# Seven-product down projection: the last weight block is copied aside, the raw buffers are released after the second e split, and the next up weights are summed behind the accumulations

## The chip, the cores and the metric

The kernel runs on one core of a Trainium2 chip. The metric is the device time of one execution in microseconds (us). Three runs of the kernel before took 1870.8, 1871.56 and 1874.53 us; the median is 1871.56 us. All rows below come from one profiled execution, with times counted from the start of its span.

A core has five engines with a queue of instructions each: TensorE (PE in the rows, with PEld for its weight loads), VectorE (DVE), ScalarE (ACT), GpSimd (POOL) and SyncE (SP). Each takes its queue in order, and an instruction whose inputs are not there holds up everything behind it on its engine. DMA transfers are issued from SP and POOL here and run on 16 DMA engines.

## The reference

One layer of an encoder on two groups of tokens (512 and 256, behind 16 shared meta tokens), in float32:

```python
def swiglu(u, wg, wu, wd):
    return (jax.nn.silu(u @ wg) * (u @ wu)) @ wd

h = h + 0.5 * swiglu(rmsnorm(h, ffn1_norm_w[layer]), ffn1_w_gate[layer], ffn1_w_up[layer], ffn1_w_down[layer])
...
h = h + jnp.concatenate([att, ssm], axis=-1) @ w_out[layer]
h = h + 0.5 * swiglu(rmsnorm(h, ffn2_norm_w[layer]), ffn2_w_gate[layer], ffn2_w_up[layer], ffn2_w_down[layer])
h = rmsnorm(h, final_norm_w)
```

The model width is 1024, the hidden width of the two SwiGLU blocks 2816. The change touches only the second one, where 768 tokens are left: some 500 us at the end of the kernel.

## The kernel before, in words

**Precision.** Every float32 weight is split into a rounded part (hi) and a rest (lo): ScalarE makes hi by a cast (L202), VectorE subtracts it from the weight (L203). A product is three matmuls: hi·hi (L372), lo·hi (L373), hi·lo (L374).

**Seven products.** The projections of the second SwiGLU are 2 x 2 block products done with seven block products, which need sums of weight blocks. One "quad" is such a block product for a pair of 128 hidden columns of gate or of up: seven steps, called here by their functions p1, p6, p5, p2, p7, p3, p4, each of 12 matmuls of 128 x 384. A quad takes two raw pieces of the weights and four split jobs: `a` (one block as it is), `b` (sums made by VectorE at L277 and L278 out of both raw pieces), `c` (a whole piece), `d` (sums at L282 and L283).

**Groups.** The hidden columns are worked in groups of two pairs. The down projection of a group is done in the middle of the next group: after the gate quad of that group's first pair comes `down_fast` for the group before, then the up quad. There are four such places, called stages 1 to 4 below. A `down_fast` goes twice over two column pairs (`cq` = 0 and 2). Each round has the products b11, b21, t2, m3, n1, b22, m4 (12 matmuls each). ScalarE puts PSUM results aside (`put`, L783), VectorE adds others to them (`fold`, L786), and each fold is followed by a DMA from POOL that adds 128 x 384 values to the residual in DRAM (L788). m4 goes on in the PSUM bank of m3 (a `ps_x` bank), so it may begin only when the fold of the m3 result has read that bank. The split jobs of a round are `e0`, `e1` (four blocks each) and `f0`, `f1` (three blocks each); f needs sums made with e, and the raw block r22.

**What sets the order.** The list `jobs` fixes the order of all weight splits, `raws_in` that of the loads: in `cq` = 2 the jobs are e0, e1, f0, f1 and then a, b, c, d of the up quad. There are two raw buffers (tag `wr`, 512 KB per load, issued from SP at L229) and four hi/lo buffers (tags `wh`, `wl`). `split` issues the next loads when a job was the last to read its raw piece; `pump` lets at most four splits run ahead of the buffers that products have freed. A recording layer then sets the instructions of each engine in a fixed order.

Of the kernel before, what the change touches and what calls it, by code (L numbers as in the profile page):

```python
# [47 lines left out]
def body(tc, x_prompt, x_sample, meta_tokens, ffn1_norm_w, ffn1_w_gate, ffn1_w_up, ffn1_w_down,  # L48
# [125 lines left out]
    def plan_down_fast(f, wd, g):  # L174
        for cq in range(0, KD // 2, 2):
            a = len(raws_in)
            for kind in "ef":
                for i in range(2):
                    jobs.append(((f, "d", g, cq + i, kind), kind + str(i), (a + i,)))
            raws_in.extend((wd, 2 * GROUPS[f][g], 4, (cq + i) * 256, 256) for i in range(2))  # L180
# [36 lines left out]
    class Weights:  # L217
        raw, ready = {}, {}
        n_dma = n_split = n_got = n_free = n_used = 0
# [16 lines left out]
        def split(self):  # L236
            j = self.n_split
            key, kind, rs = jobs[j]
            while self.n_dma <= max(rs):
                self.dma()  # L240
# [20 lines left out]
        def split_fast(self, key, kind, raw, hi, lo):  # L261
# [6 lines left out]
            if kind[0] in "ef":  # L268
                return self.split_down(key, kind, raw[0], hi, lo)
            hv, lv = (t.rearrange("p a b -> p (a b)").rearrange("p (s k f) -> p s k f", s=2, k=4) for t in (hi, lo))  # L270
            if kind == "a":
                ins = split(hv[:, 0], lv[:, 0], raw[0][:, :, x])
            else:
                if kind == "b":
                    sums = stretch_pool[0].tile([P, 2 * 4 * P], F32, tag="sums", name="sums", bufs=1)
                    t = self.sums = sums.rearrange("p (s k f) -> p s k f", s=2, k=4)
                    V.tensor_tensor(t[:, 1], raw[0][:, :, y], raw[1][:, :, y], ALU.add)  # L277
                    V.tensor_tensor(t[:, 0], t[:, 1], raw[0][:, :, x], ALU.add)  # L278
                else:

                    t, self.sums = self.sums, None
                    V.tensor_tensor(t[:, 1], raw[0][:, :, x], raw[0][:, :, y], ALU.add)  # L282
                    V.tensor_tensor(t[:, 0], t[:, 0], raw[1][:, :, x], ALU.add)  # L283
                ins = split(hv, lv, t)
# [3 lines left out]
        def split_down(self, key, kind, r, hi, lo):  # L288

            x, y = slice(0, P), slice(P, 2 * P)  # L290
            r11, r12, r21, r22 = r[:, 0:2, x], r[:, 2:4, x], r[:, 0:2, y], r[:, 2:4, y]
            hv, lv = (t.rearrange("p a b -> p (a b)").rearrange("p (s k f) -> p s k f", s=4, k=2) for t in (hi, lo))
            odd = kind[1] == "1"
            if kind[0] == "e":
# [14 lines left out]
                split(hv[:, 2:4], lv[:, 2:4], s23)  # L309
                n = 4  # L310
            else:
                ins = split(hv[:, 0:2], lv[:, 0:2], self.sumb if odd else self.sums[:, 2:4])
                split(hv[:, 2], lv[:, 2], r22)
                n = 3
# [3 lines left out]
            return ins  # L318

        def pump(self, most=1):  # L320
            while most and self.n_split < min(len(jobs), self.n_free + NHL):
                self.split()
                most -= 1
# [227 lines left out]
    def ffn(f, h, halves, norm, after, last, new_g, new_up, first, parts=None, rms=None, ended=None, kept=None):  # L551
# [219 lines left out]
        def down_fast(g, late):  # L771
# [13 lines left out]
            def fold(t, src, m, hf):  # L785
                V.scalar_tensor_tensor(t, src[:, :n0], 0.5, t, ALU.mult, ALU.add)  # L786
                o, n = halves[hf]
                G.dma_start(out=kept[m][:, o:o + n], in_=t, accum_op=ALU.add)  # L788

            for cq in range(0, KD // 2, 2):  # L790
                two = range(2)
                e = [W.get((f, "d", g, cq + i, "e")) for i in two]
                m0 = [2 * (cq + i) for i in two]
# [33 lines left out]
                for i in two:  # L827
                    z.append(ps_mm())
                    prod(z[i], fs[i][1], "b22")
                    fold(c12[i], z[i], m0[i], 1)  # L830
                    done()
# [1075 lines left out]
```

## Time and profile before

| | |
|---|---|
| median of three runs | 1871.56 us |
| profiled execution, own time | 1870.07 us |
| its span, first to last instruction | 1868.3 us |
| TensorE busy | 1787.5 us (96%) |
| VectorE busy | 1353.1 us (72%) |
| ScalarE busy | 850.0 us (45%) |

The profiled execution is 1.5 us shorter than the median of the runs. TensorE is busy nearly throughout, so what counts is where it is not, and where its granted clock is below full speed (a lower clock counts as busy). A row of a timeline has the start, the length, the engine, the line, the operation, output and input names, and in square brackets how long the engine sat idle before it and what ended that.

### The profile page before, as it was taken

Reading aid. Unit: us, or ns where it says so; the run is one execution under the profiler, and the core shown is the slowest. Engines: PE = TensorE matmul, PEld = TensorE weight load, DVE = VectorE, ACT = ScalarE, POOL = GpSimd, SP = SyncE. Lnnn points to the kernel's source line nnn. Section 1 sums busy time; section 2 is a strip of 40 time slices with the busy share of each in tenths; the row PEclk is TensorE's granted clock in tenths of the full one; section 3 lists DMA queues with packets and bytes.
Section 4 is the critical chain, followed back from the end, with each engine's and each line's share of the span. In section 5 each row is a group of like instructions: output and inputs, shape, how many; then the busy total and the mean of one; then the engine's idle time right before and its main releaser. Section 6 shows DMA issues by size and latency. Waiting matters only on the chain. (4 is left out here: it accounts for less than half of the span.)

```text
span 1868.3 us, 27750 instructions
## 1 busy us (share of the span) xinstructions
PE 1787.5 (96%) x10622; PEld 1708.1 (91%) x10622; DVE 1353.1 (72%) x2679; ACT 850.0 (45%) x1700; POOL 159.0 (9%) x198
## 2 busy tenths in 40 slices
PE   8999999999999999998999999999999898989898
PEld 7999999999999987887988989999999898989897
DVE  6857858585864796767787887756878585858663
ACT  6513414142433535766476764533435353434434
POOL 0000000000020000323000000003001102020302
PEclk9999999999999999998999999999999999999999
DMA  4212212121232525965432135221232525262631
GB/s 142 74 46 74 80 54 83 48 88 46 91 116 60 155 82 141 258 184 160 149 103 72 60 126 188 80 68 46 76 103 72 122 76 116 68 124 68 147 124 68
DMA packets 171767, 188.65 MB, mean 101 GB/s; under 512 B 11201, under 2 KB 155706, under 8 KB 171634
## 3 DMA queue, kind: packets, MB, share of 16 engines
q1 hardware_dynamic: 161122, 168.00, 29.9%
q0 software_dynamic: 10496, 18.88, 5.3%
q8 instruction: 83, 1.36, 0.3%
q14 instruction: 50, 0.41, 0.1%
q10 hardware_dynamic: 16, 0.00, 0.0%
HBM read 151.68 MB, written 38.60 MB: 102 GB/s over the span
## 5 line engine op out<-in xcount | busy, mean ns | idle before, releaser
L372 PE MATMUL ps_mm<-w,wh 128*128 128x384 f32 (+4 forms) x1200 | 408.9, 341 | 9.3 <-DVE f L679 2.8
L373 PE MATMUL ps_mm<-w,wl 128*128 128x384 f32 (+4 forms) x1200 | 405.9, 338 | 1.5 <-DVE wl L203 1.5
L374 PE MATMUL ps_mm<-w,wh 128*128 128x384 f32 (+4 forms) x1160 | 393.6, 340 | 2.7 <-DVE w L203 2.2
L202 ACT CAST wh<-wr 128x512 fp32r<-128x512 f32 (+1 forms) x210 | 182.2, 867 | 182.5 <-PE ps_x L374 90.6
L203 DVE TENSOR_TENSOR wl<-wr,wh 128x512 fp32r<-128x512 f32 (+1 forms) x210 | 210.4, 1002 | 54.8 <-ACT wh L202 53.2
L372 PEld LDWEIGHTS ps_mm<-w,wh 128*128 128x128 f32 x1200 | 226.4, 189 | 17.9 <-issue 4.5
L373 PEld LDWEIGHTS ps_mm<-w,wl 128*128 128x128 f32 x1200 | 226.3, 189 | 4.7 <-DVE wl L203 2.2
L374 PEld LDWEIGHTS ps_mm<-w,wh 128*128 128x128 f32 x1160 | 218.7, 189 | 7.5 <-DVE w L203 3.0
L202 ACT CAST wh<-sums 128x1024 fp32r<-128x1024 f32 (+1 forms) x100 | 94.7, 947 | 201.3 <-DVE sums L278 85.5
L372 PE MATMUL ps_x<-w,wh 128*128 128x392 f32 (+4 forms) x432 | 150.4, 348 | 22.2 <-DVE f L786 21.3
L372 PE MATMUL ps_s<-w,wh 128*128 128x384 f32 (+1 forms) x432 | 148.7, 344 | 9.7 <-DVE f L673 7.5
L373 PE MATMUL ps_x<-w,wl 128*128 128x392 f32 (+4 forms) x432 | 147.8, 342 | 0.0
L373 PE MATMUL ps_s<-w,wl 128*128 128x384 f32 (+1 forms) x432 | 147.2, 341 | 0.0
L374 PE MATMUL ps_s<-w,wh 128*128 128x384 f32 (+1 forms) x432 | 146.8, 340 | 0.0
L203 DVE TENSOR_TENSOR wl<-sums,wh 128x1024 fp32r<-128x1024 f32 (+1 forms) x100 | 109.6, 1096 | 42.3 <-ACT wh L202 42.2
L374 PE MATMUL ps_x<-w,wh 128*128 128x392 f32 (+4 forms) x392 | 134.5, 343 | 0.0
L421 POOL TENSOR_TENSOR w<-w,w 128x392 f32<-128x392 f32 (+3 forms) x36 | 41.7, 1160 | 1009.7 <-ACT w L420 1009.7
L372 PEld LDWEIGHTS ps_x<-w,wh 128*128 128x128 f32 x432 | 84.6, 196 | 25.6 <-DVE f L786 22.9
L372 PEld LDWEIGHTS ps_s<-w,wh 128*128 128x128 f32 x432 | 82.2, 190 | 14.3 <-DVE f L673 9.8
L373 PEld LDWEIGHTS ps_x<-w,wl 128*128 128x128 f32 x432 | 84.6, 196 | 0.7
L373 PEld LDWEIGHTS ps_s<-w,wl 128*128 128x128 f32 x432 | 82.0, 190 | 0.0
L374 PEld LDWEIGHTS ps_s<-w,wh 128*128 128x128 f32 x432 | 81.8, 189 | 0.0
(408 smaller groups left out, 3951.1 us busy)
## 6 DMA issues: line engine op xcount, KB each, us to landing
wr<-in_ffn_w_gate_dram SPq DMA_DIRECT2D x44, 512.0 KB
wr<-in_ffn_w_up_dram SPq DMA_DIRECT2D x42, 512.0 KB
wr<-in_w_in_dram SPq DMA_DIRECT2D x42, 512.0 KB
wr<-in_ffn_w_down_dram SPq DMA_DIRECT2D x40, 512.0 KB
w<-ar_d SPq DMA_DIRECT2D x24, 512.0 KB
wr<-in_w_out_dram SPq DMA_DIRECT2D x16, 512.0 KB
w<-ar_d SPq DMA_DIRECT2D x24, 256.0 KB
w<-q_d SPq DMA_DIRECT2D x32, 192.0 KB
```

The lines of the kernel that those rows point to most:

```text
L202: a = S.copy(hi, src)
L203: return a, V.tensor_tensor(lo, src, hi.bitcast(F32), ALU.subtract)
L372: nc.tensor.matmul(ps, ah, bh, start=start, stop=False, skip_group_check=onto)
L373: nc.tensor.matmul(ps, al, bh, start=False, stop=False, skip_group_check=onto)
L374: last_mm[0] = nc.tensor.matmul(ps, ah, bl, start=False, stop=stop, skip_group_check=onto)
L421: G.tensor_tensor(sums[0], sums[0], sq, ALU.add)
```

## The change

It has two parts, and both stand in `down_fast` and its weight splits.

First, the raw pieces of a round are needed by e0 and e1 alone. After e1, ScalarE copies the two raw blocks r22 (128 x 256 each) into the sums tile, in the place of sums that are split by then, and the f jobs split r22 from there. The f jobs name no raw piece any more; the piece of e0 is kept until the copies.

Second, in the round `cq` = 2 the job `b` of the next up quad is held back until both c12 folds are recorded, and its first addition is told to stand behind the second of them.

```diff
@@ plan_down_fast
-                    jobs.append(((f, "d", g, cq + i, kind), kind + str(i), (a + i,)))
+                    rs = ((a,), (a, a + 1))[i] if kind == "e" else ()
+                    jobs.append(((f, "d", g, cq + i, kind), kind + str(i), rs))
@@ Weights.split
-            while self.n_dma <= max(rs):
+            while rs and self.n_dma <= max(rs):
@@ Weights.split_fast
-                return self.split_down(key, kind, raw[0], hi, lo)
+                return self.split_down(key, kind, raw[-1] if raw else None, hi, lo)
...
                 if kind == "b":
+                    if self.behind:
+                        kept_order = behind([self.behind])
+                        self.behind = None
+                    else:
+                        kept_order = ExitStack()
                     sums = stretch_pool[0].tile([P, 2 * 4 * P], F32, tag="sums", name="sums", bufs=1)
                     t = self.sums = sums.rearrange("p (s k f) -> p s k f", s=2, k=4)
-                    V.tensor_tensor(t[:, 1], raw[0][:, :, y], raw[1][:, :, y], ALU.add)
+                    with kept_order:
+                        V.tensor_tensor(t[:, 1], raw[0][:, :, y], raw[1][:, :, y], ALU.add)
@@ Weights.split_down
                 split(hv[:, 2:4], lv[:, 2:4], s23)
                 n = 4
+                self.r22.append(r22)
+                if odd:
+                    for i in range(2):
+                        S.copy(s23[:, i], self.r22[i])
+                    self.r22 = []
             else:
                 ins = split(hv[:, 0:2], lv[:, 0:2], self.sumb if odd else self.sums[:, 2:4])
-                split(hv[:, 2], lv[:, 2], r22)
+                split(hv[:, 2], lv[:, 2], self.sums[:, int(odd)])
@@ Weights.pump
-            while most and self.n_split < min(len(jobs), self.n_free + NHL):
+            while most and self.n_split != self.hold and self.n_split < min(len(jobs), self.n_free + NHL):
@@ down_fast
             for cq in range(0, KD // 2, 2):
                 two = range(2)
+                if cq:
+                    W.hold = W.n_got + 5
...
-                    fold(c12[i], z[i], m0[i], 1)
+                    W.behind = fold(c12[i], z[i], m0[i], 1)
+                    if i:
+                        W.hold = None
                     done()
```

In the rows of the changed kernel the lines have moved: L203 is L205, L277 and L278 are L285 and L286, L282 and L283 are L290 and L291, L673 is L692, L679 is L698, L689 is L708, L697 is L716, L783 is L802, L786 is L805.

VectorE, second round of stage 1, from the c11 folds (`f<-ps_s`) on; `f<-ps_x` are the folds of the m3 results, `w<-ps_mm` the c12 folds, `w<-ps_x` the folds of m4; `wl<-wr 128x512` is the lo part of the up quad's `a`, and the sums are those of its `b` and `d`. Before:

```order
L786 SCALAR_TENSOR_TENSOR f_14271<-ps_s,f_14271 128x384 x2
L277 TENSOR_TENSOR sums<-wr 128x512
L278 TENSOR_TENSOR sums<-sums,wr 128x512
L203 TENSOR_TENSOR wl<-wr,wh 128x512
L203 TENSOR_TENSOR wl<-sums,wh 128x1024
L786 SCALAR_TENSOR_TENSOR f_14342<-ps_x,f_14342 128x384 x2
L786 SCALAR_TENSOR_TENSOR w_14343<-ps_mm,w_14343 128x384
L282 TENSOR_TENSOR sums<-wr 128x512
```

Now:

```order
L805 SCALAR_TENSOR_TENSOR f_14275<-ps_s,f_14275 128x384 x2
L205 TENSOR_TENSOR wl<-wr,wh 128x512
L805 SCALAR_TENSOR_TENSOR f_14339<-ps_x,f_14339 128x384 x2
L805 SCALAR_TENSOR_TENSOR w_14340<-ps_mm,w_14340 128x384 x2
L285 TENSOR_TENSOR sums<-wr 128x512
L805 SCALAR_TENSOR_TENSOR w_14306<-ps_x,w_14306 128x384
L286 TENSOR_TENSOR sums<-sums,wr 128x512
L805 SCALAR_TENSOR_TENSOR w_14306<-ps_x,w_14306 128x384
L205 TENSOR_TENSOR wl<-sums,wh 128x1024
L205 TENSOR_TENSOR wl<-wr,wh 128x1024
L290 TENSOR_TENSOR sums<-wr 128x512
L291 TENSOR_TENSOR sums<-sums,wr 128x512
```

The sums of `b`, which need both raw pieces of the up weights, stood ahead of the m3 folds and stand behind the c12 folds now; one lo part, which needs the first raw piece, is ahead of the m3 folds still.

ScalarE, the same round, from the last three puts of the first round (`cq` = 0) to the first of the second (`w<-ps_s` and `f<-ps_s` are puts, the casts those of e1, f0 and f1 of `cq` = 2). Now:

```order
L802 ACTIVATE f_14205<-ps_s 128x384
L204 CAST wh<-sums 128x512
L802 ACTIVATE w_14206<-ps_s 128x384
L324 COPY sums<-wr 128x256 x2
L204 CAST wh<-sums 128x512
L204 CAST wh<-sums 128x256
L204 CAST wh<-sumb 128x512
L204 CAST wh<-sums 128x256
L802 ACTIVATE f_14275<-ps_s 128x384 x2
```

The two copies stand between the last put of the first round and the casts of the f jobs, whose 128x256 ones read `sums` where they read `wr`.

VectorE a little later in stage 1, in the up quad; L673/L692 takes up the result of p6, L679/L698 that of p5, L689/L708 that of p2, and the last `wl<-wr 128x512` and `sums<-wr` belong to `a` and `b` of the next gate quad. Before:

```order
L203 TENSOR_TENSOR wl<-sums,wh 128x1024
L203 TENSOR_TENSOR wl<-wr,wh 128x512
L673 TENSOR_TENSOR f_14412<-f_14412,ps_s 128x384
L277 TENSOR_TENSOR sums<-wr 128x512
L278 TENSOR_TENSOR sums<-sums,wr 128x512
L679 TENSOR_TENSOR f_14413<-ps_mm,f_14412 128x384
```

Now:

```order
L692 TENSOR_TENSOR f_14416<-f_14416,ps_s 128x384
L205 TENSOR_TENSOR wl<-sums,wh 128x1024
L698 TENSOR_TENSOR f_14417<-ps_mm,f_14416 128x384
L205 TENSOR_TENSOR wl<-wr,wh 128x512
L708 TENSOR_TENSOR w_13925<-ps_s,w_13925 128x384
L285 TENSOR_TENSOR sums<-wr 128x512
```

The results of p6 and p5 stood behind instructions that wait for the next gate weights and stand ahead of them now; the result of p2 is behind the first of these instructions.

## Rows read from the trace of the kernel before

**Rows 1.** The page's first part: busy time, share of the span and instructions of each engine.

```profile
span 1868.3 us, 27750 instructions
PE 1787.5 (96%) x10622; PEld 1708.1 (91%) x10622; DVE 1353.1 (72%) x2679; ACT 850.0 (45%) x1700; POOL 159.0 (9%) x198
```

**Rows 2.** The waits of TensorE from 1455 us to the end: who waited, for what, us in total, times, longest.

```profile
PE ps_x L372 <- DVE f L786: 21.3, 5, 5.6
PE ps_s L372 <- DVE f L673: 7.5, 7, 2.6
PE ps_mm L372 <- DVE f L679: 2.8, 2, 2.4
```

**Rows 3.** TensorE's timeline in stage 1: the last matmul of b22, the first of m4, the first of the up quad (p1).

```profile
1459.18 0.34 PE L374 MATMUL ps_mm<-w,wh 128*128 128x384 f32 x1
1464.82 0.69 PE L372 MATMUL ps_x<-w,wh 128*128 128x384 f32 x1 [5.30 <-DVE f L786]
1468.82 0.34 PE L372 MATMUL ps_s<-w,wh 128*128 128x384 f32 x1
```

**Rows 4.** TensorE in stretches: from:to and length, busy us (instructions), granted clock as a share of full speed, DMA share, GB/s. The first six are the stretches at the lower clock in the four stages; the last is undisturbed.

```profile
1461.97:1468.80 6.83, 3.98 (x12) 0.50 0.37 46
1560.96:1567.79 6.83, 4.15 (x13) 0.50 0.32 40
1663.36:1666.77 3.41, 3.41 (x13) 0.50 0.51 66
1677.01:1680.42 3.41, 3.41 (x12) 0.50 0.01 2
1762.35:1769.17 6.82, 5.68 (x18) 0.50 0.53 84
1782.83:1786.24 3.41, 3.41 (x13) 0.50 0.05 7
...
1500.00:1542.00 42.00, 42.00 (x242) 1.00 0.29 80
```

**Rows 5.** VectorE's timeline in stage 1 around the m3 folds.

```profile
1460.46 0.69 DVE L277 TENSOR_TENSOR sums<-wr 128x512 f32<-128x512 f32 x1 [8.69 <-DMA wr<-in_ffn_w_up_dram]
...
1463.07 1.23 DVE L203 TENSOR_TENSOR wl<-sums,wh 128x1024 fp32r<-128x1024 f32 x1 [0.59 <-ACT wh L202]
1464.21 1.01 DVE L786 SCALAR_TENSOR_TENSOR f<-ps_x,f 128x384 f32<-128x384 f32 x2
```

**Rows 6.** All waits of the kernel, the two lines of VectorE on raw weights.

```profile
DVE sums L277 <- DMA wr<-in_ffn_w_up_dram: 38.1, 9, 9.0
...
DVE sums L277 <- DMA wr<-in_ffn_w_gate_dram: 23.2, 15, 5.0
```

**Rows 7.** The DMA issues of stage 1 on SP (up, then gate weights, then the next up weights; a row with x2 merges two issues of 0.37 us, the second at its end) and on POOL (the additions to the residual).

```profile
1447.63 1.77 SPq L229 DMA_DIRECT2D wr<-in_ffn_w_up_dram  x2
1466.35 4.75 SPq L229 DMA_DIRECT2D wr<-in_ffn_w_gate_dram  x2
1483.53 4.66 SPq L229 DMA_DIRECT2D wr<-in_ffn_w_up_dram  x2
...
1444.74 1.72 POOL L788 DMA_DIRECT2D hh_d<-f  x2 [6.31 <-DVE f L786]
```

**Rows 8.** Stretches of stage 1 as in rows 4; the last two columns are the mean busy share of the DMA engines and GB/s.

```profile
1442.50:1446.00 3.50, 3.50 (x21) 1.00 0.00 0
1446.00:1459.50 13.50, 13.50 (x77) 1.00 1.06 193
1459.50:1466.00 6.50, 1.20 (x5) 0.69 0.01 2
1466.00:1477.50 11.50, 11.20 (x56) 0.88 1.00 194
```

**Rows 9.** ScalarE's timeline in stage 1: a put, the casts of f0 and the first cast of the up weights.

```profile
1443.38 0.48 ACT L783 ACTIVATE w<-ps_s 128x384 f32<-128x384 f32 x1
1445.92 0.62 ACT L202 CAST wh<-sums 128x512 fp32r<-128x512 f32 x1 [2.06 <-PE ps_x L374]
1446.44 0.40 ACT L202 CAST wh<-wr 128x256 fp32r<-128x256 f32 x1
...
1454.82 0.62 ACT L202 CAST wh<-wr 128x512 fp32r<-128x512 f32 x1 [1.09 <-DMA wr<-in_ffn_w_up_dram]
```

**Rows 10.** VectorE's timeline in stage 1, in the up quad and in the gate quad after it.

```profile
1474.49 0.69 DVE L203 TENSOR_TENSOR wl<-wr,wh 128x512 fp32r<-128x512 f32 x1 [2.65 <-ACT wh L202]
1475.10 0.55 DVE L673 TENSOR_TENSOR f<-f,ps_s 128x384 f32<-128x384 f32 x1
1478.56 0.69 DVE L277 TENSOR_TENSOR sums<-wr 128x512 f32<-128x512 f32 x1 [2.92 <-DMA wr<-in_ffn_w_gate_dram]
...
1491.61 0.69 DVE L277 TENSOR_TENSOR sums<-wr 128x512 f32<-128x512 f32 x1 [0.67 <-DMA wr<-in_ffn_w_up_dram]
```

**Rows 11.** Stage 4: the waits of TensorE from 1755 to 1800 us; SP's gate loads; VectorE's sums that wait for them.

```profile
PE ps_mm L372 <- DVE f L679: 2.4, 1, 2.4
PE ps_s L372 <- DVE f L673: 0.8, 2, 0.6
...
1765.03 4.79 SPq L229 DMA_DIRECT2D wr<-in_ffn_w_gate_dram  x2
...
1780.00 0.69 DVE L277 TENSOR_TENSOR sums<-wr 128x512 f32<-128x512 f32 x1 [4.99 <-DMA wr<-in_ffn_w_gate_dram]
```

More of the change, by code (lines that the diff above doesn't have):

```diff
@@ L217, in body @@
     class Weights:
-        raw, ready = {}, {}
+        raw, ready, r22 = {}, {}, []
         n_dma = n_split = n_got = n_free = n_used = 0
@@ L290, in split_down @@
             x, y = slice(0, P), slice(P, 2 * P)
-            r11, r12, r21, r22 = r[:, 0:2, x], r[:, 2:4, x], r[:, 0:2, y], r[:, 2:4, y]
+            if r is not None:
+                r11, r12, r21, r22 = r[:, 0:2, x], r[:, 2:4, x], r[:, 0:2, y], r[:, 2:4, y]
             hv, lv = (t.rearrange("p a b -> p (a b)").rearrange("p (s k f) -> p s k f", s=4, k=2) for t in (hi, lo))
@@ L318, in split_down @@
             return ins
+        hold = None
+        behind = None
         def pump(self, most=1):
-            while most and self.n_split < min(len(jobs), self.n_free + NHL):
+            while most and self.n_split != self.hold and self.n_split < min(len(jobs), self.n_free + NHL):
                 self.split()
@@ L785, in fold @@
             def fold(t, src, m, hf):
-                V.scalar_tensor_tensor(t, src[:, :n0], 0.5, t, ALU.mult, ALU.add)
+                ins = V.scalar_tensor_tensor(t, src[:, :n0], 0.5, t, ALU.mult, ALU.add)
                 o, n = halves[hf]
                 G.dma_start(out=kept[m][:, o:o + n], in_=t, accum_op=ALU.add)
+                return ins
             for cq in range(0, KD // 2, 2):
                 two = range(2)
+                if cq:
+                    W.hold = W.n_got + 5
                 e = [W.get((f, "d", g, cq + i, "e")) for i in two]
```

## The prediction

> **What bounds the kernel now.** I read the page's first part, then the waits of TensorE, then the timelines of one stage, engine by engine. TensorE is busy for 1787.5 of 1868.3 us and no other engine is near that [rows 1], so the reader has to look for the places where it is not. From the first of the four down stages on they are few: five waits of 21.3 us in all for the fold of L786, four of them about 5 us and one of 0.2, and nine shorter ones, 7.5 + 2.8 = 10.3 us, for L673 and L679 [rows 2]. In stage 1 the long one lies between the last product of b22 and the first of m4: 5.30 us [rows 3].
>
> A wait has a second price. Behind each long one the granted clock is 0.50, the lower of its two levels (1.2 of 2.4 GHz), and 12 matmuls take 3.98 us; at full clock 242 take 42.00 us, so 12 take 2.08 [rows 4]. TensorE is busy at the low clock for 3.98, 4.15, 3.41 and 5.68 us behind the four long waits, 17.2 us in all, of which half is lost: 8.6 us. Two more low stretches, behind shorter waits in stages 3 and 4, lose half of 6.8: 3.4 us [rows 4]. All of it together, 21.3 + 10.3 + 8.6 + 3.4 = 43.6 us, is what this change can reach.
>
> Why does m4 wait? VectorE's timeline shows it: its queue stands 8.69 us at L277, the first sum of the up quad's `b`, for the second raw piece of the up weights, and the m3 fold, whose inputs are long there, comes behind it at 1464.21 [rows 5]. The same pair is the longest wait of VectorE on raw weights [rows 6]. The piece is late since its load is issued second, at 1447.63 + 1.77 - 0.37 = 1449.03 [rows 7], when a raw buffer is free, and since the DMA engines are full from 1446 to 1459.5 with this load and the additions to the residual, then idle while TensorE waits [rows 8].
>
> **The change, part by part.** *The order on VectorE.* With `b` behind the c12 folds, only one waiting instruction is ahead of the m3 folds, the lo part of `a`. It needs the first raw piece, which is there at 1454.82 already before [rows 9]. n1 ends at some 1457.3 (b22 has 12 products of 0.174 us and ends at 1459.5, rows 3 and 4), so its puts and the m3 folds are done by 1459 and m4 starts at 1459.4 with no gap. This takes away the 21.3 us and the 8.6 us of clock: 29.9.
>
> *What is late next.* `b` now begins after the second c12 fold, whose product ends at 1459.5 [rows 3]; with 0.5 us for the fold, L285 starts at about 1460.05. From the start of L277 to the end of its lo part the trace has 1463.07 + 1.23 - 1460.46 = 3.84 us [rows 5], and a fold of m4 (half of 1.01 us) now stands between the two sums: the lo part is ready at 1464.4. TensorE does m4 and p1 in 24 x 0.174 = 4.2 us and wants it at 1463.8, the second matmul after 1463.6. That is a new wait of 0.6 us a stage if the raw piece is there by 1460, too short for the clock as far as the rows go; I take 0.5, 2 us for four stages. Bounds: nothing, if VectorE and ScalarE follow each other closer than in the rows, and 1.0 us a stage, if the piece still lands at 1460.46 as now [rows 5].
>
> *The loads.* The copies stand where ScalarE has 2.06 us idle, after the put of 1443.38 [rows 9]. They wait for the lo part of e1's sums, some 1445, and take 0.40 us each, by the cast of the same 128 x 256 [rows 9]; so they end near 1446.0, when the next cast came anyway, and 16 copies (6.4 us) cost TensorE nothing. If that cover were gone they would delay the puts of c11 by 0.8 us a round, 6.4 us at most. The up loads can then go out at about 1445.7 and 1446.1, 2 and 3 us before, into DMA engines that are idle until 1446 [rows 8]. I expect the second piece at some 1458, before its sum is allowed to start.
>
> The rows show the second piece landing 11.4 us after its issue while additions fill the engines [rows 5, 7, 8]. The Trainium skill, "DMA: Bandwidth & Descriptors", section "Queues, rings and completion order", has two rules that pull apart here: an engine takes packets from its queues in turn, which lets an earlier load finish earlier, but a semaphore's increment lands only after every earlier write of that engine, of other queues too, which speaks against the change, since the load would be told done only with the additions ahead of it. By the second rule the piece stays at 1460.4, `b` starts 0.4 us later than I said, and the sum is 1.6 us smaller; by the first it is as I have it.
>
> *The gate weights after it.* Their loads go out when L282 and L283 (now L290, L291) have read the raw buffers: before at 1466.35 and 1466.35 + 4.75 - 0.37 = 1470.73 [rows 7], the second held by the lo part of `c`. Now `c` is ahead of these sums, and all is done at about 1466.5 (1464.4 plus 1.2, 0.6 and 0.6), so both go at about 1466. TensorE is 7.4 us further on, though: it wants `a` of the gate quad at 1474.5 and, behind L285, the p7 result for p4 at 1476.6. Two bounds for the landing: 7.5 us, as for the first gate load under additions (1466.35 to about 1473.8, rows 7 and 10), and 3.8 us on idle engines (the up load of 1483.53 + 4.66 - 0.37 = 1487.82 lands at 1491.61, rows 7 and 10). The additions of this round start some 7 us earlier and need 11.5 us together with 1 MB of loads [rows 8], so they are nearly over at 1468. I take a landing of the second piece at 1472 to 1474: no wait in stages 1 to 3.
>
> *The short waits.* They come from results of p6 and p5 behind VectorE's stops for gate and up weights, as L673 behind the lo part at 1474.49 and L679 behind L277 at 1478.56 [rows 10]. In the new order both stand ahead of those stops. Of the 10.3 + 3.4 = 13.7 us I count stages 1 to 3 as gone and stage 4 as kept: 2.4 + 0.8 us of waits and 1.7 of clock [rows 4, 11], since there the eight reloads of the residual go through the same engines, and the second gate piece came 1780.0 - 1769.45 = 10.5 us after its issue [rows 11]. That is 13.7 - 4.9 = 8.8 us gained.
>
> **The sum.** 29.9 + 8.8 - 2.0 = 36.7 us off 1870.07 gives 1833.4 in the profiled execution; the median of the runs lies 1.5 above it, so 1835.
>
> **The rivals.** *The gate weights become the wait.* What speaks for it: TensorE reaches them 7.4 us sooner and their issue moves by 0.4 and 4.7 us only. Against it: the engines were idle for 6.5 us just before [rows 8], and that work moves forward. If they land half way between my guess and the old times, p4 waits about 2 us in every stage, and the short waits come back in another place: 29.9 - 2 - 8 = 20 us gained, 1852. If they keep their old times, p4 waits 4.3 us and the clock falls again, 6 us a stage: 1867.
>
> *The m3 fold still waits.* The lo part of `a` is ahead of it, and if the first up piece came after 1457.5 nothing would be won: 1871. It landed at 1454.8 from a later issue [rows 9]; only if both pieces came together could it be so.
>
> *Slower.* One mechanism: in the gate quad the p2 and p7 results (L708, L716) now stand behind the lo part of `a` and L285, so each late microsecond of a gate load is one of TensorE. From a second piece at about 1482 on, 15.5 us after its issue, it costs more than the 7.4 us that a stage wins, and at 1485 three more in each of the four stages, 12 over the time before: 1883. Nothing in the rows takes over 11.4 us [rows 5, 7].
>
> **How the numbers follow.** Forecast, faster by 25 to 45 us: 0.76. Gate weights partly in the way, faster by 5 to 25: 0.15. The fold still waits, or all given back, no change: 0.05. Slower: 0.04. What a measurement here can tell from no change is about 0.2%, 3.7 us. So faster 0.91, same 0.05, slower 0.04. The range reaches from all 43.6 us gained with no new wait (1828), and 2 us below that for restarts of TensorE that I did not count, to the first rival's 1852 with 2 us more: 1826 to 1854.
>
> **What would show it.** The long wait of `ps_x` L372 for the fold (now L805) gone from TensorE's waits; no granted clock of 0.50 behind m4; L285 not waiting for a DMA in the up quad; up loads issued about 2 us before, as a pair 0.4 to 0.6 us apart, and gate loads as a pair too. A wait of TensorE of about 0.5 us at the start of p6 or p5 for the lo part of `b` would confirm the new chain. I am wrong if TensorE waits some microseconds at p1 or p4 of the gate quad in stages 1 to 3, or if ScalarE's puts come later behind the copies.

## The result and the profile after

The changed kernel takes 1838.49 us (median of six runs, 1835.32 to 1841.49) against 1871.18 us for the kernel before in the same runs: a ratio of 0.9825, 95% interval 0.981 to 0.9841, some 32.7 us less. The forecast was 1835 in a range of 1826 to 1854. The profiled execution took 1835.32 us, the shortest of the six.

The page's first part [rows 1]:

```profile
span 1833.6 us, 27768 instructions
PE 1775.7 (97%) x10622; PEld 1699.9 (93%) x10622; DVE 1353.3 (74%) x2679; ACT 855.4 (47%) x1716; POOL 156.8 (9%) x198
```

The span is 34.7 us shorter. TensorE's busy time fell by 11.8 us with the same 10622 instructions: mostly matmuls that no longer run at the lower clock. ScalarE has the 16 copies more. TensorE's waits from 1455 us to the end, as in [rows 2]:

```profile
PE ps_s L391 <- DVE f L692: 4.0, 4, 1.2
PE ps_x L391 <- DVE f L716: 2.5, 1, 2.5
PE ps_mm L392 <- DVE wl L205: 1.4, 4, 0.4
PE ps_s L391 <- ACT wh L204: 1.1, 1, 1.1
...
PE ps_s L392 <- DVE wl L205: 0.3, 1, 0.3
```

The line of 21.3 us for the fold is gone. (L372 to L374 are L391 to L393 in the changed kernel, L229 is L231; each edit below shifts the lines a little again.) In stage 1 TensorE passes from the last matmul of b22 to the first of m4 and on to p1 without a gap, where [rows 3] had 5.30 us:

```profile
1458.47 0.34 PE L393 MATMUL ps_mm<-w,wh 128*128 128x384 f32 x1
1458.65 0.34 PE L391 MATMUL ps_x<-w,wh 128*128 128x384 f32 x1
...
1460.77 0.34 PE L391 MATMUL ps_s<-w,wh 128*128 128x384 f32 x1
```

Of the six stretches at the lower clock [rows 4] one is left, in stage 4 (from:to and length, then TensorE's, its weight loads', VectorE's, ScalarE's and POOL's busy us, the granted clock, the DMA share, GB/s):

```profile
1751.37:1754.78 3.41, 3.41 (x12) 3.41 (x11) 3.41 (x5) 1.59 (x3) 0.00 (x0) 0.50 0.00 0
```

VectorE in stage 1, as in [rows 5]:

```profile
1456.24 0.56 DVE L805 SCALAR_TENSOR_TENSOR f<-ps_x,f 128x384 f32<-128x384 f32 x1 [1.30 <-DMA hh_d<-f]
1457.28 0.56 DVE L805 SCALAR_TENSOR_TENSOR f<-ps_x,f 128x384 f32<-128x384 f32 x1 [0.49 <-ACT f L802]
...
1459.40 0.68 DVE L285 TENSOR_TENSOR sums<-wr 128x512 f32<-128x512 f32 x1
1459.99 0.55 DVE L805 SCALAR_TENSOR_TENSOR w<-ps_x,w 128x384 f32<-128x384 f32 x1
...
1462.26 1.23 DVE L205 TENSOR_TENSOR wl<-sums,wh 128x1024 fp32r<-128x1024 f32 x1 [0.65 <-ACT wh L204]
```

The m3 folds run at 1456.24 and 1457.28 instead of 1464.21. The addition L285 has no bracket: its raw piece is there when its turn comes, where L277 stood 8.69 us. From 1455 us to the end VectorE no longer waits for up weights at all; before it did so seven times, for 36.3 us.

The kept-back job has work on ScalarE too, the cast of its sums. Before, ScalarE stood at that cast, waiting for the sums, and n1's puts came behind it:

```profile
1461.99 1.04 ACT L202 CAST wh<-sums 128x1024 fp32r<-128x1024 f32 x1 [6.54 <-DVE sums L278]
1462.94 0.48 ACT L783 ACTIVATE f<-ps_s 128x384 f32<-128x384 f32 x1
```

Now the puts come as soon as n1 has ended, and the cast behind them:

```profile
1455.71 0.49 ACT L802 ACTIVATE f<-ps_s 128x384 f32<-128x384 f32 x1 [1.50 <-PE ps_s L393]
...
1461.18 1.05 ACT L204 CAST wh<-sums 128x1024 fp32r<-128x1024 f32 x1 [3.55 <-DVE sums L286]
```

The m3 fold adds to what such a put has written. So with ScalarE in the old order the fold had to come behind the sums, whatever VectorE's order was: the wait for the up piece held it up on two engines.

Loads and copies [rows 7, 9]:

```profile
1444.41 1.11 SPq L231 DMA_DIRECT2D wr<-in_ffn_w_up_dram  x2
1465.29 1.57 SPq L231 DMA_DIRECT2D wr<-in_ffn_w_gate_dram  x2
```

```profile
1443.98 0.71 ACT L324 COPY sums<-wr 128x256 f32<-128x256 f32 x2 [0.56 <-DVE wl L205]
1453.59 0.62 ACT L204 CAST wh<-wr 128x512 fp32r<-128x512 f32 x1 [0.56 <-PE ps_x L393]
```

Both loads go out as pairs (the second issue of each, 0.64 and 0.96 us long, ends the row): up at 1444.41 and 1444.88, gate at 1465.29 and 1465.89. VectorE's wait for gate weights from 1455 us on fell from 12.9 us to 3.4 (the 23.2 us of [rows 6] are those of the whole kernel). The first three of stage 4's waits come from the gate loads; the last is the one for L692 that the earlier stages have too:

```profile
DVE sums L285 <- DMA wr<-in_ffn_w_gate_dram: 3.4, 5, 2.0
```

```profile
1745.17 0.44 PE L391 MATMUL ps_s<-w,wh 128*128 128x384 f32 x1 [1.13 <-ACT wh L204]
1745.90 0.45 PE L392 MATMUL ps_s<-w,wl 128*128 128x384 f32 x1 [0.29 <-DVE wl L205]
1750.55 0.45 PE L391 MATMUL ps_x<-f,wh 128*128 128x384 f32 x1 [2.45 <-DVE f L716]
1759.84 0.44 PE L391 MATMUL ps_s<-w,wh 128*128 128x384 f32 x1 [1.22 <-DVE f L692]
```

**The account.** Waits of TensorE in these stages: 31.6 us before, 9.3 after, 22.3 gained. Clock: half of 24.0 us before, half of 3.41 after, 10.3 gained. Together 32.6 of the 34.7 us by which the spans differ. The rest lies largely ahead of the stages: the same event, TensorE's wait of some 0.5 us for a split weight near 1336 us, stands at 1337.42 in the profile before and at 1335.98 after.

### The profile page after: what moved, and what is told of

It reads as the page before. It is cut to its first block, busy times and chain, and to the rows that moved or that the text cites. A ratio compares the mean times of both kernels' runs of the same rounds, so it can differ in the third digit from the quotient of the medians.

```text
span 1833.6 us, 27768 instructions
## 1 busy us (share of the span) xinstructions
PE 1775.7 (97%) x10622; PEld 1699.9 (93%) x10622; DVE 1353.3 (74%) x2679; ACT 855.4 (47%) x1716; POOL 156.8 (9%) x198
## 4 chain that ended last, share of the span: by engine, by line
PE 75%; DVE 13%; DMA 5%; ACT 4%; issue 2%; POOL 0%; SPq 0%; DVEq 0%; POOLq 0%; ACTq 0%
PE ps_mm L392 11%; PE ps_mm L391 11%; PE ps_mm L393 11%; PE ps_x L391 7%; PE ps_x L393 7%; PE ps_x L392 7%; PE ps_s L391 5%; PE ps_s L392 5%; PE ps_s L393 5%; DVE wl L205 2%; DVE w L1272 2%; DMA wr<-in_ffn_w_gate_dram 2%; PE ps_s L1712 2%; PE ps_s L1830 1%; DMA w<-ar_d 1%
## 5 line engine op out<-in xcount | busy, mean ns | idle before, releaser
L391 PE MATMUL ps_mm<-w,wh 128*128 128x384 f32 (+4 forms) x1200 | 409.0, 341 | 6.3 <-DVE w L1591 2.1
L393 PE MATMUL ps_mm<-w,wh 128*128 128x384 f32 (+4 forms) x1160 | 393.6, 340 | 2.7 <-DVE w L205 2.2
L204 ACT CAST wh<-wr 128x512 fp32r<-128x512 f32 (+1 forms) x194 | 175.5, 905 | 171.6 <-PE ps_x L393 92.8
L205 DVE TENSOR_TENSOR wl<-wr,wh 128x512 fp32r<-128x512 f32 (+1 forms) x194 | 203.8, 1051 | 63.3 <-ACT wh L204 61.7
L391 PEld LDWEIGHTS ps_mm<-w,wh 128*128 128x128 f32 x1200 | 226.8, 189 | 13.8 <-issue 4.4
L393 PEld LDWEIGHTS ps_mm<-w,wh 128*128 128x128 f32 x1160 | 218.9, 189 | 7.2 <-DVE w L205 2.8
L204 ACT CAST wh<-sums 128x1024 fp32r<-128x1024 f32 (+2 forms) x116 | 100.2, 870 | 173.7 <-PE ps_x L393 70.5
L391 PE MATMUL ps_s<-w,wh 128*128 128x384 f32 (+1 forms) x432 | 147.5, 341 | 8.4 <-DVE f L692 4.7
L205 DVE TENSOR_TENSOR wl<-sums,wh 128x1024 fp32r<-128x1024 f32 (+2 forms) x116 | 115.6, 1003 | 42.4 <-ACT wh L204 41.4
L391 PE MATMUL ps_x<-w,wh 128*128 128x392 f32 (+4 forms) x432 | 146.0, 338 | 0.9 <-ACT w L1354 0.9
L393 PE MATMUL ps_s<-w,wh 128*128 128x384 f32 (+1 forms) x432 | 146.1, 338 | 0.0
L393 PE MATMUL ps_x<-w,wh 128*128 128x392 f32 (+4 forms) x392 | 131.0, 334 | 0.0
L391 PEld LDWEIGHTS ps_s<-w,wh 128*128 128x128 f32 x432 | 81.0, 188 | 12.7 <-DVE f L692 6.3
L391 PEld LDWEIGHTS ps_x<-w,wh 128*128 128x128 f32 x432 | 82.0, 190 | 2.3 <-ACT w L1354 1.2
L1736 ACT ACTIVATE w<-w,nmx 128x528 f32<-128x528 f32 (+1 forms) x96 | 63.6, 663 | 40.0 <-DVE nmx L1732 31.1
```

The costliest lines, as they stand in the source:

```text
L204: a = S.copy(hi, src)
L205: return a, V.tensor_tensor(lo, src, hi.bitcast(F32), ALU.subtract)
L391: nc.tensor.matmul(ps, ah, bh, start=start, stop=False, skip_group_check=onto)
L393: last_mm[0] = nc.tensor.matmul(ps, ah, bl, start=False, stop=stop, skip_group_check=onto)
L1736: S.activation(e[:, :nk], e[:, :nk], AF.Exp, bias=nmx[:, c:c + 1], scale=-1.0, accum_out=(s0, s1)[c])
```

## The experiments

Between profiles the time ahead of that event differs by up to 8 us (1331.8 to 1340.0), in code that no edit touches or hardly touches. So the table has, beside the ratio of the runs, the profiled time from that event to the end of the span. This column has noise of its own, and each kernel has one profile: from the event to the first fold of stage 1, where six of these kernels (the changed one, copies only, copies at the old place, first fold, late reloads, both) run the same instructions, they take 98.7 to 100.0 us. A difference of up to 1.4 us in the last column therefore says nothing, and one of 2 to 3 us little by itself. The kernel before took 1867.6 to 1871.2 us in the sets of runs that the medians come from; each ratio is to the kernel before of the same set.

| kernel | ratio to before (95%) | median us | event to end, us |
|---|---|---|---|
| before | 1 | 1871.18 | 530.9 |
| changed | 0.9825 (0.981 to 0.9841) | 1838.49 | 497.6 |
| order only | 0.982 (0.9802 to 0.9838) | 1835.73 | 500.1 |
| copies only | 1.0059 (1.0037 to 1.0081) | 1880.95 | 536.0 |
| copies, old place | 0.9937 (0.9912 to 0.9962) | 1858.67 | 521.1 |
| before + 24 matmuls into y | 1.0026 (1.0013 to 1.004) | 1873.13 | 536.3 |
| before + b22 five times | 0.9965 (0.9953 to 0.9976) | 1864.11 | 525.6 |
| changed, first fold | 0.9825 (0.98 to 0.985) | 1837.71 | 498.9 |
| changed, late reloads | 0.9789 (0.9764 to 0.9813) | 1831.98 | 489.8 |
| both of these | 0.9796 (0.9775 to 0.9818) | 1832.53 | 491.9 |
| both, x and y apart | 0.9747 (0.973 to 0.9764) | 1822.05 | 483.8 |
| the same, no copies | 0.9764 (0.9747 to 0.9781) | 1824.99 | 487.8 |
| late reloads, x and y apart | 0.9747 (0.9725 to 0.9769) | 1823.23 | 483.3 |
| the same, no copies | 0.9752 (0.973 to 0.9774) | 1824.14 | 486.3 |

Diffs are against the changed kernel where nothing else is said.

### Order only

```diff
-rs = ((a,), (a, a + 1))[i] if kind == "e" else ()
+rs = (a + i,)
...
-S.copy(s23[:, i], self.r22[i])
...
-split(hv[:, 2], lv[:, 2], self.sums[:, int(odd)])
+split(hv[:, 2], lv[:, 2], r22)
```

> The changed kernel without the two copies: the seventh-block jobs read the raw pieces again, so these come free where they did before; the additions for the next up products still stand behind the second of the two folds of c12. Theory (the order of VectorE makes the gain, the earlier loads only keep the wait from coming back): the up loads are issued near 1447.6 and 1449 us again, the second lands near 1460.4, so the first addition stands at 1460.5 instead of 1459.4; the four waits of some 5 us ahead of the m4 products and the half clock behind them stay away, the wait of the second up product for its split grows from 0.35 to about 1.4 us in each stage, some 4 us in all: 1842 to 1845 us. Rival (the early release makes the gain): the long waits come back in another place, behind additions that wait for their piece: 1860 us or more.

Measured: 0.982, the whole gain. A wait of TensorE, and VectorE at the addition:

```profile
PE ps_mm L386 <- DVE wl L205: 2.8, 4, 0.8
```

```profile
1457.67 0.69 DVE L285 TENSOR_TENSOR sums<-wr 128x512 f32<-128x512 f32 x1 [0.72 <-DMA wr<-in_ffn_w_up_dram]
```

The second piece, issued at 1445.83, lands 0.72 us too late for its addition, and the wait for the split is 0.8 instead of 0.35 us in stages 1 to 3; the theory had the direction, but 1.4 us. The price is smaller than expected: 2.5 us from the event to the end, 1.5 of it this wait, and none that the runs show. The gain is the order's, that is of keeping the job `b` back as a whole, with its addition on VectorE and its cast on ScalarE; the two were not tried apart.

### Copies only

```diff
-W.hold = W.n_got + 5
...
-W.behind = fold(c12[i], z[i], m0[i], 1)
-if i:
-    W.hold = None
+fold(c12[i], z[i], m0[i], 1)
```

> The changed kernel without the hold and without the ordering behind the fold: the copies stay and release the raw pieces early, the additions for the next ups stand where they stood before the change, ahead of the folds of c12. Up loads are issued near 1444.4 and 1444.9 us. Theory (order makes the gain; the second up piece lands at 1458 to 1459.4 because the additions into memory share the DMA engines): VectorE still stands at the first addition with the folds behind it, each long wait falls by only 1 to 2.5 us, the half clock behind it stays: 1861 to 1867 us. Rival (the early release alone does it): the piece lands by 1455 us, before the folds are due, the long waits and the half clock are gone and no new wait appears: 1836 to 1841 us.

Measured: 1.0059, slower than the kernel before. Both theories missed this. VectorE and a wait of TensorE:

```profile
1449.87 0.56 DVE L805 SCALAR_TENSOR_TENSOR f<-ps_s,f 128x384 f32<-128x384 f32 x1 [1.19 <-PE ps_s L393]
1458.11 0.69 DVE L285 TENSOR_TENSOR sums<-wr 128x512 f32<-128x512 f32 x1 [7.69 <-DMA wr<-in_ffn_w_up_dram]
1458.72 0.55 DVE L805 SCALAR_TENSOR_TENSOR f<-ps_s,f 128x384 f32<-128x384 f32 x1
```

```profile
PE ps_s L391 <- DVE f L805: 25.1, 4, 7.5
```

The program's order came out differently here: the addition moved up to between the two folds of c11. The raw piece does not land until 1458.1, so now a fold of c11 stands behind it too, and TensorE waits 7.45 us for that one, earlier in the stage. An early load gives nothing when an instruction that waits for it is ahead of work that TensorE waits for. By the code the product that waits, the second of t2, goes on in x and the fold reads y, the other half of the same PSUM tile: it is no wait on data. Two tiles were not tried in this place.

### Copies, with the additions at their old place

The kernel of the run before, and the additions told to stand behind the second c11 fold, where they were before the change.

```diff
-fold(c11[i], y[i], m0[i], 0)
+ins = fold(c11[i], y[i], m0[i], 0)
+if cq and i:
+    W.behind = ins
```

> Copies only again, with the additions for the next ups held behind the second fold of c11, which is exactly where VectorE had them before the change (in the run with copies alone they had moved up by one more fold). The up loads come some 3 us earlier than before, and that is the only difference. Theory (place on VectorE decides, the loads matter only for how long the engine stands there): the second up piece lands at about 1457.6 us instead of 1460.5, the four long waits fall from some 5.3 to 2.5 us and part of the half clock behind them goes: 8 to 17 us faster than before, a ratio of 0.991 to 0.995, and not near the 0.982 of the order alone. Rival (early release is worth as much as the order): 0.983 or less. Second rival (the landing is set by the additions into memory, not by the issue): no change, 0.998 to 1.002.

Measured: 0.9937, as the theory had it.

```profile
1459.65 0.69 DVE L285 TENSOR_TENSOR sums<-wr 128x512 f32<-128x512 f32 x1 [5.32 <-DMA wr<-in_ffn_w_up_dram]
```

```profile
PE ps_x L391 <- DVE f L805: 12.7, 4, 4.7
```

VectorE stands 5.32 us instead of 8.69, and the long waits are 12.7 instead of 21.3 us. Against the common event (2.55 us later in this profile) the second load goes out 3.4 us earlier than before, at 1448.14, and the piece lands 3.4 us earlier. So the copies alone are worth a third of the gain, the order alone all of it, and the two do not add.

### Work in the wait

The kernel before, with matmuls whose results are not read, ahead of the m4 products.

```diff
+if cq:
+    for j in range(24):
+        nc.tensor.matmul(y[1][:, :n0], fs[1][1][0][0], gb["b22"][0][0], start=True, stop=True)
```

> The kernel before, with 24 more matmuls of 128x384 in each of the four stages, ahead of the m4 products, into a half of the sums' PSUM buffer that is free there; their results are not read. They take some 24 x 0.173 = 4.2 us and lie in a wait of 5 us. Theory (8.6 us of the reachable time is clock: TensorE runs at 1.2 GHz for a stretch behind each long wait): the wait ahead of the m4 products shrinks to about 1 us, TensorE stays at 2.4 GHz behind it, and the kernel comes out 7 to 9 us faster than before: 1862 to 1864 us. Rival (the half clock is not due to the idle time, or costs nothing since VectorE is late there anyway): 1868 to 1873 us. If the matmuls did not fit into the wait they would add up to 17 us: 1880 us or more.

Measured: 1.0026. The experiment missed its aim:

```profile
1464.13 6.63 PE L834 MATMUL ps_s<-w,wh 128*128 128x384 f32 x24 [4.43 <-ACT w L783]
```

```profile
1461.51 1.04 ACT L202 CAST wh<-sums 128x1024 fp32r<-128x1024 f32 x1 [6.36 <-DVE sums L278]
...
1463.58 0.50 ACT L783 ACTIVATE w<-ps_s 128x384 f32<-128x384 f32 x1
```

The added matmuls did not fill the wait, they waited themselves, for ScalarE's last put. That put reads x, they write y; the two are halves of one PSUM tile, and the program orders its accesses tile by tile. (The put is late since it stands behind the cast of the up sums: the addition held ScalarE too.) What it shows of the clock is still of use: the 24 took 6.47 us, most of it at the lower clock, and m4 behind them ran at the full one.

### The same with a product made five times

In the kernel before, the second b22 product of the round is made five times, each beginning anew.

```diff
-prod(z[i], fs[i][1], "b22")
+for again in range(5 if cq and i else 1):
+    prod(z[i], fs[i][1], "b22")
```

> The kernel before, with the second b22 product of each stage made five times over into the same PSUM tile (each begins anew, so the last one stands): 24 more matmuls, some 24 x 0.173 = 4.2 us, which wait for nothing and lie in the wait ahead of the m4 products (5.3 us); the fold that reads the tile stands behind the additions on VectorE until later than that. Theory (the half clock follows from TensorE's idle time and costs 1.9 us in the m4 products alone): the wait falls to about 1 us, TensorE stays at 2.4 GHz behind it, and though waits of up to 2 us further on take part of it back the kernel is 3 to 8 us faster: a ratio of 0.9955 to 0.9985. Rival (the clock costs nothing since VectorE is late behind it anyway): 0.999 to 1.002. If the added work counted in full: 17 us slower, 1.009.

Measured: 0.9965, 6.75 us faster with 96 matmuls more. TensorE's waits, one of them, and the only stretch at the lower clock left in the stages:

```profile
PE ps_s L372 <- DVE f L673: 13.2, 7, 3.7
PE ps_x L372 <- DVE f L786: 4.4, 4, 1.5
```

```profile
1478.23 0.44 PE L372 MATMUL ps_s<-w,wh 128*128 128x384 f32 x1 [3.67 <-DVE f L673]
```

```profile
1479.66:1483.07 3.41, 3.41 (x13) 3.41 (x12) 2.54 (x4) 1.04 (x1) 0.00 (x0) 0.50 0.00 0
```

The long waits shrink from 21.3 to 4.4 us and the full clock holds behind them, where the kernel before has 24.0 us at the lower one in the stages and this one 3.41. So the fall of the clock follows from the idle time. But 5.7 us of what is saved come back as waits for L673 (7.5 before): VectorE is late there whatever TensorE does.

### Behind the first fold

```diff
-W.behind = fold(c12[i], z[i], m0[i], 1)
-if i:
-    W.hold = None
+ins = fold(c12[i], z[i], m0[i], 1)
+if not i:
+    W.behind, W.hold = ins, None
```

> The changed kernel with the additions for the next ups behind the first of the two folds of c12 instead of the second, one place (0.56 us) earlier on VectorE. Theory: the waits of the second up product for its split (four of 0.32 to 0.37 us) go, nothing else is late since the second fold's PSUM buffer is not asked for until later: 1 to 1.5 us less than the changed kernel, a ratio to before of 0.981 to 0.982, which only the trace tells from no change. Rival (the addition meets its piece not yet landed there and the second fold stands behind it): a wait on the fold of some 1 us per stage, 2 to 4 us slower than the changed kernel.

Measured: 0.9825, and 1.3 us more from the event to the end, which is within that column's noise.

```profile
PE ps_s L391 <- DVE f L692: 5.9, 4, 2.4
PE ps_s L391 <- ACT wh L204: 4.4, 1, 4.4
```

The four waits for the split are gone, as the theory had it, but TensorE waits longer for the gate weights of stage 4 (4.4 us instead of 1.1 and 2.5) and for L692 (5.9 instead of 4.0), and stage 4 has two stretches at the lower clock instead of one. It comes sooner, and the first gate piece, though issued 2.6 us earlier (1732.66 instead of 1735.25), is cast 1.0 us later (1745.54 instead of 1744.50). So there was no new wait at the fold, and no gain.

### Late reloads

```diff
 h[m] = w3(n0 + n1)
-G.dma_start(out=h[m], in_=kept[m])
+W.reload.append((h[m], kept[m]))
...
+if self.n_dma == len(raws_in) - 4:
+    with behind([ins]):
+        for o, i in self.reload:
+            nc.sync.dma_start(out=o, in_=i)
```

> The changed kernel with the eight reloads of the residual, which the POOL queue issued between 1722 and 1741 us, moved to SP's queue behind the last up loads (some 1756 us). Theory (the two waits of stage 4 on the gate weights, 1.13 and 0.29 us, the wait of 2.45 us behind the first addition and the half clock after it come from the reloads sharing the DMA engines with the gate loads): the gate pieces land some 4 us after issue as in stages 1 to 3, these waits go, the clock stays: 4 to 6 us less than the changed kernel, a ratio to before of 0.979 to 0.980. Rival (the gate loads are late because of their issue at 1735 us, or of the additions into memory): 0.982 to 0.983. If the reloads come too late for the last down products, whose first sum is due at 1788 us, a new wait of up to 10 us appears there.

Measured: 0.9789, and 7.8 us less from the event to the end (1.4 of it ahead of the stages, where the two kernels are the same), a little more than expected either way. ScalarE's cast of the first gate piece of stage 4:

```profile
1739.37 0.62 ACT L204 CAST wh<-wr 128x512 fp32r<-128x512 f32 x1 [3.05 <-DMA wr<-in_ffn_w_gate_dram]
```

The piece lands 4.7 us after its issue at 1734.65; in the changed kernel it took from 1735.25 to 1744.50, 9.25 us. In stage 4 only the new wait of 0.35 and the one for L692 (0.96) are left, no stretch is at the lower clock, and no wait for the residual appears.

### Both, and then two tiles

The two edits above in one kernel:

> The changed kernel with both edits that were tried apart: additions behind the first fold of c12, and the residual reloads behind the last up loads. Theory (the gain of the first was there but was given back in stage 4, where TensorE waits for the gate weights whenever it comes, and with the reloads out of the way it stays): no wait for a split behind the folds, no wait in stage 4, only the four waits of about 1 us on the sum that reads the second up product; 1 to 2 us less than with the late reloads alone, a ratio to before of 0.977 to 0.9785. Rival (the waits of about 1 us grow by what is saved, since VectorE is behind there): 0.9785 to 0.980, as with the late reloads alone.

Measured: 0.9796, and 2.1 us more than late reloads alone, 1.1 of it ahead of the stages: the rival. One line has most of it:

```profile
PE ps_s L396 <- DVE f L697: 7.1, 4, 2.1
```

The waits for L697 (L692 of the changed kernel) grew from 4.3 to 7.1 us, while the four waits for the split, 1.4 us, went. So that wait was next to be tried:

```diff
-st["x"], st["y"] = S2[:, 0], S2[:, 1]
+st["x"], st["y"] = S2[:, 0], ps_s()[:, 0] if f == 2 else S2[:, 1]
```

> As the kernel with both edits, and in the second feed-forward part the two products x and y of a quad lie in two PSUM tiles instead of the two halves of one. Theory (the fourth product of a quad, which goes on in x, waits for the VectorE sum that reads y only because both lie in one tile): the four waits of about 1 us are gone, 3 to 5 us less than without this edit, a ratio to before of 0.9745 to 0.976. Rival (VectorE is behind there in any case, so that the wait comes back one or two products later): the waits are named after another line and the ratio stays at 0.977 to 0.9785.

Measured: 0.9747, 8 us less than without this edit. The largest waits left from 1450 us to the end:

```profile
PE ps_s L396 <- ACT f L807: 0.7, 2, 0.5
PE ps_x L396 <- DVE f L721: 0.6, 1, 0.6
PE ps_s L396 <- DVE f L810: 0.5, 3, 0.2
```

The wait for the sum that reads y was one for the tile only. The quads between the event and stage 1 gain by it too: 2.7 us of waits on the common tile went there. This is the fastest kernel of the study by its median, 1822.05 us.

Then the same kernel without the copies, by the diff of the run with the order alone:

> As the kernel with two PSUM tiles and both edits, but without the copies of the seventh block: the raw pieces come free as in the kernel before. Theory (the copies bring 2 to 3 us of earlier landing, which the order of the changed kernel does not need but the earlier place behind the first fold does): the second up piece lands some 1.5 to 2 us after VectorE comes to the addition, the second fold of c12 and the folds behind it stand for that time, and a wait of 0.5 to 1.5 us per stage comes back: 2 to 6 us slower than with the copies. Rival (the copies are worth nothing in any of these orders): within 1.5 us of it.

Measured: 0.9764, and 4 us more from the event to the end.

```profile
1452.81 0.69 DVE L290 TENSOR_TENSOR sums<-wr 128x512 f32<-128x512 f32 x1 [1.34 <-DMA wr<-in_ffn_w_up_dram]
```

```profile
PE ps_s L391 <- DVE wl L205: 2.8, 4, 0.8
```

Without the copies VectorE stands at the addition and the four waits for the split come back. The intervals of the two ratios overlap; only the trace tells them apart, by these waits.

The next has late reloads and two tiles, without the edit on the first fold:

> As the fastest kernel so far (late reloads, x and y of a quad in two PSUM tiles, additions behind the first fold of c12), with the additions behind the second fold again, as in the changed kernel. Theory (the place one fold earlier is worth the four waits of 0.35 us, now that nothing takes them back): these waits return, 1 to 2 us slower than behind the first fold, from TensorE's wait for a split near 1336 us to the end some 485 us instead of 483.8. Rival (the earlier place only moves work on VectorE and gains nothing, as in the run where it stood alone): 483 to 484 us.

Measured: 0.9747 and 483.3 us, the rival: the place one fold earlier is worth nothing that these numbers show. By the event to the end, late reloads and two tiles take 14 us off the changed kernel.

```profile
PE ps_s L396 <- ACT f L807: 1.2, 2, 0.6
PE ps_s L397 <- DVE wl L205: 0.7, 4, 0.2
```

And that one without the copies:

> As the kernel before in this list, without the copies of the seventh block. Theory (the copies are worth the 0.45 us by which the second up piece lands too late for its addition, in each stage, as in the run with the order alone): waits of 0.7 to 0.8 us instead of 0.35 for the second up product's split, 1.5 to 2.5 us slower than with the copies. Rival (they are worth nothing): the same within 0.5 us from TensorE's wait near 1336 us to the end. Second rival (worth as much as behind the first fold): 4 us slower.

Measured: 0.9752, which the runs can't tell from the kernel with copies, and 3 us more from the event to the end. The waits for the split are 2.0 us in all instead of 0.7. That is a little more than expected; of the other 1.7 us, 0.7 lie ahead of the stages and the rest is open.

## Why the prediction was right, and where it was not

*The order on VectorE, 29.9 us.* Right in size, and right that an addition which waits for its load was ahead of the fold. The order alone gives all the gain; the m3 folds run with no gap behind n1's puts; no low clock stands behind m4. But I read the m3 fold's inputs as "long there", and they were not: n1's first put began at 1462.94, behind the cast of the same sums on ScalarE. Moving the folds on VectorE alone would not have been enough. The change keeps back the whole job, cast included; I had not worked that out, and in this the forecast was lucky. The clock's part, 8.6 us, was real: with the waits filled and the full clock kept, the kernel before was 6.75 us faster though it did more work. But it can't be banked by itself, since waits for L673 took 5.7 us back.

*The copies and the loads.* That the copies cost nothing held (they run at 1443.98, in idle time, and the up loads go out 1.3 us earlier than I said). That the earlier loads were needed did not: without the copies the piece comes only 0.72 us late in stage 1. From the event to the end that kernel takes 2.5 us more; in the two orders that were tried later the difference is 4 and 3 us, and the longer waits for the split are 1.3 to 2.8 us of these. I had worked this out as my bound (1.0 us a stage if the piece still lands as before) and not drawn the conclusion that the first part of the change is worth next to nothing beside the second.

*What lands when.* The Trainium skill, "DMA: Bandwidth & Descriptors", section "Queues, rings and completion order", had two rules, and I had let one of them hold the piece at 1460.4 us. It did not stay: in the run with copies at the old place it moved with its issue, 3.4 us for 3.4 us, and with copies alone 2.0 us for 3.4. That does not refute the other rule, since the additions to the residual landed earlier in these runs as well. In the kernel before, with the order alone, with copies alone and with copies at the old place VectorE went on 0.1 to 0.3 us after an addition had landed (in the kernel before at 1460.46, with the addition at 1460.39), as it would if the load were told done behind that addition. Which rule sets the landing stays open.

*The new wait.* Predicted 0.5 us a stage, measured 0.32 to 0.37.

*The short waits, 8.8 us.* This step failed. I counted those of stages 1 to 3 as gone because L673 would stand ahead of the stops for raw weights. It does, but in the gate quad of a stage's second pair it stands behind other work of VectorE, the lo part of the next `a` last, and 2.8 us stayed there (0.81, 1.08 and 0.92; 1483.23 in stage 1). I read this wait as one on data. The product that waits goes on in x, the sum reads y, and only the common tile joins them: with two tiles it is gone. By the code the 7.5 us for L673 before the change are waits of the same kind; two tiles were not tried in that kernel. Stage 4 kept more than I allowed: 1.13 + 0.29 + 2.45 + 1.22 us of waits and 1.7 of clock, 6.8 instead of 4.9. So the step gave 8.8 - 2.8 - 1.9 = 4.1 us. The cause I named for stage 4, the reloads in the same DMA engines, is shown for the first three of these waits and for the clock, which went when the reloads were moved; the 1.22 us are the wait on the common tile again (0.96 stayed then, and went with two tiles).

*The gate weights.* Issues at 1465.29 and 1465.89 (forecast: both near 1466; the times it adds up come to 1466.8, not 1466.5), and the second piece holds VectorE for 0.35 us at 1471.36, a little ahead of the 1472 to 1474 forecast. The first rival did not come about in stages 1 to 3; in stage 4 it did, as a wait at p1 and at p4, for the reason that set it apart.

The sum: 29.9 + 4.1 - 1.4 = 32.6 us, against 36.7 forecast. The profiled execution gave 34.7 less for the span, 2.1 of it unaccounted for here, and it lies 3.2 us under its own median, where I had taken 1.5 from the kernel before. The forecast is 3.5 us too low because the short waits were taken 4.7 us too well and the medians stand 1.7 us further from their profiles; the new wait (0.6) and the 2.1 us go the other way.

## What to carry to other kernels

When an engine in program order stands at an instruction that waits for a load, look first at what is queued behind it, there and on every engine that waits for its result; moving that work gave here the whole gain, and hurrying the load a third of it, or a loss where the earlier load drew its user forward. Take a wait's name as a question: is it on the data, or on a tile that two results share? And when a saving disappears, follow it to the next wait: here it went to stage 4's loads and then to a shared tile, and came out once both were gone.

## What was not expected

A load of 512 KB behind the additions to the residual lands 11.4 to 12.8 us after its issue: 11.4 before, 11.5 with copies at the old place (1448.14 to 1459.65), 11.8 with the order alone (1445.83 to 1457.67), 12.8 with copies alone (1445.30 to 1458.11). Against the common event, an issue 3.4 us earlier came back as a landing 3.4 us earlier in one run and 2.0 in the other.

In the kernel before, the addition held two engines: ScalarE's puts stood behind the cast of the sums that it makes (6.54 us idle, and 6.36 in the run with matmuls into y). The prediction had only VectorE's queue.
